# Two layers of a hybrid attention encoder: which of the engines beside TensorE splits the weights, scales the softmax rows and multiplies the norm

## The chip, the cores and the metric

The kernel runs on one core of one Trainium2 chip. The metric is the device time of one execution in microseconds (us). A core has TensorE (PE: matrix products, whose results lie in PSUM; PEld: its weight loads), VectorE (DVE), ScalarE (ACT), GpSimd (POOL) and SyncE (SP), which here issues the DMAs. Each engine works through its own queue in order, and engines wait for each other by semaphores.

## The reference

Batch 1, 512 rows, width 1024, two layers, all in f32. Cut to what matters:

```python
for l in range(DEPTH):
    mod = (silu(c) @ w_ada[l] + b_ada[l]).reshape(B, 9, D_MODEL)
    h = rms_norm(x) * (1 + mod[1]) + mod[0]
    x = x + 0.5 * mod[2] * swiglu(h, w_gate, w_up, w_down)              # first FFN
    h = rms_norm(x) * (1 + mod[4]) + mod[3]
    qa, ka, va, ub, qc, kc, vc, f, g = split(h @ w_in)                  # the mixer
    ya = attention(norm(qa), norm(ka), va, bias by distance, own + 8 chunks of 64)   # 8 heads of 64
    yb = trailing-window means of ub, minus ub, through w_pool
    yc = attention(norm(qc), norm(kc), vc, bias cumsum(log_sigmoid(f)), causal)      # 8 heads of 64
    x = x + mod[5] * (sum_n sigmoid(g_n) * (y_n @ w_branch[n])) @ w_out
    h = rms_norm(x) * (1 + mod[7]) + mod[6]
    x = x + 0.5 * mod[8] * swiglu(h, w_gate, w_up, w_down)              # second FFN
```

## The kernel before

Activations lie transposed: 128 channels on the partitions, 512 rows of the sequence as columns. To hold f32 precision every operand is split into a high part of a shorter type (fp32r) and a low part (`lo = value - hi`), and each product is three matmuls (`triple`, L119 to L121: high by high, high by low, low by high). So every weight chunk (128x1024 f32, 512 KB, DMA by SP) goes through `wchunk`: ACT casts the high part (`whi`, L268), and one engine subtracts for the low part (`wlo`, L270). `LO_SHARE = 1` gives the subtraction to POOL for the chunks loaded during the two attentions and to DVE elsewhere; `= 0` gives all to DVE there.

A layer is first FFN, mixer, second FFN. Each of the six begins with an RMS norm (`Norm`) in two halves of 256 columns. The squares are summed on ACT and POOL; PE sums over partitions; DVE makes the inverse root by three Newton steps (`rsqrt`, L276 to L284); PE spreads it over the partitions (`rb`, in PSUM), and ACT copies that to SBUF (`rbs`, L353). Then come eight pieces a half (`piece`): multiply by the inverse root (DVE from PSUM for three of eight, L360; POOL from `rbs` for five, L362), ACT's high part `hhi` (L364), DVE's low part `hlo` (L365). The products that follow read `hhi` and `hlo`.

In the mixer come the projections (`proj`), attention A, attention C, the pooling branch, the gates and the output. The query and key projections (`proj_qk`) end in a norm by head: DVE sums squares, `rsqrt` on 128x32, then for each of four row blocks a 128x512 multiplication by the inverse root (L665, two on POOL and two on DVE), then transposes on PE (`turn`).

An attention (`attention`) goes head by head, four query blocks of 128 each, in four steps:

- `logits`: PE products (L777, L778); DVE adds the bias strip and takes the row maximum (L781); ACT's exponential with row sums (L785); DVE reciprocal (L787); DVE scales the probabilities by it (`t<-t,rs`, L788).
- `turn`: PE transposes the scaled rows (L800), ACT copies the high part (L804), DVE subtracts the low part (L805).
- `weigh`: PE multiplies with the values (L822, L823); ACT and DVE add the halves (L826, L827), then `split_to` (L375 on ACT, L376 on DVE) writes the two parts of `y`.
- The strips of C come by DMA for a head ahead; POOL adds the causal mask to their diagonal blocks (L763).

Between these steps PE is given other products ("filler": projections and gates). What stands where is decided when the program is built: `pe[0]` counts PE time, `later(delay, fn)` notes a step to be emitted when `pe[0]` passes its due time, and `poll()` emits what is due. `LAG_T`, `LAG_V`, `STEP`, `TURN` are such delays. Tiles of one name share few buffers (`t1` has two, `t2` three, `strip` two), so that a step may wait until an older tile is read.

Of the kernel before, what the change touches and what calls it, by code (L numbers as in the profile page):

```python
# [15 lines left out]
F32 = mybir.dt.float32  # L16
# [3 lines left out]
ALU = mybir.AluOpType  # L20
# [20 lines left out]
def encoder_kernel(tc, xT, c, w_ada, b_ada, gains, w_gate, w_up, w_down, w_qkv, w_f, w_ubg,  # L41
# [22 lines left out]
    def st(shape, dt, tag, bufs):  # L64
        return sb.tile(shape, dt, tag=tag, bufs=bufs, name=nm(tag))
# [205 lines left out]
        return hi, lo  # L271


    def rsqrt(v, n):
        jt = st([P, n], I32, "nt_j", 2)
        nc.vector.tensor_scalar(jt, v.bitcast(I32), -0.5, 1597463007.0, op0=ALU.mult, op1=ALU.add)  # L276
        y = jt.bitcast(F32)
        for _ in range(3):
            q = st([P, n], F32, "nt_q", 1)
            u = st([P, n], F32, "nt_u", 1)  # L280
            z = st([P, n], F32, "nt_z", 2)
            nc.vector.tensor_tensor(q, y, y, op=ALU.mult)
            nc.vector.scalar_tensor_tensor(u, q, -0.5, v, op0=ALU.mult, op1=ALU.mult)  # L283
            nc.vector.scalar_tensor_tensor(z, u, 1.5, y, op0=ALU.add, op1=ALU.mult)  # L284
            y = z
        return y

    def xd(d):
        return x_blocks[d // 2][:, d % 2, :]
# [4 lines left out]
    class Norm:  # L294
# [10 lines left out]
        def sq(self, d, hs):  # L305

            cols = slice(0, T) if hs is None else slice(hs * HALF, (hs + 1) * HALF)
            x = xd(d)[:, cols]
            n = cols.stop - cols.start
            if d == 0:  # L310
                nc.scalar.activation(self.ssum[:, cols], x, AF.Square)
            elif d < KD - 1:
                q = t1(T)[:, :n]
                nc.scalar.activation(q, x, AF.Square)  # L314
                nc.gpsimd.tensor_tensor(self.ssum[:, cols], self.ssum[:, cols], q, op=ALU.add)  # L315
            else:
                self.work[hs] = st([P, 3 * HALF], F32, "strip", 2)
                w = self.work[hs][:, :HALF]
                nc.scalar.activation(w, x, AF.Square)
                nc.vector.tensor_tensor(w, w, self.ssum[:, cols], op=ALU.add)  # L320
            if d % 2 == 0 and self.xa[d // 2] is None:
                self.xa[d // 2] = blk(self.xtag, F32)
            nc.scalar.activation(self.xa[d // 2][:, d % 2, cols], x, AF.Identity, scale=apre[:, self.l, self.s, d:d + 1])
# [20 lines left out]
        def back_start(self, hs, bank):  # L344
            if self.state[hs] > 1:
                return
            self.front(hs, bank)
            self.state[hs] = 2
            w = self.work[hs]
            rb = bank((P, HALF))  # L350
            mm(rb, ones, w[:, HALF:2 * HALF], start=True, stop=True)
            rbs = w[:, 2 * HALF:3 * HALF]
            nc.scalar.copy(rbs, rb)  # L353
            cols = slice(hs * HALF, (hs + 1) * HALF)

            def piece(d):
                b = modc[:, self.l, 3 * self.s, d:d + 1]
                t = self.xa[d // 2][:, d % 2, cols]
                if d in ON_DVE:
                    nc.vector.tensor_tensor(t, rb, t, op=ALU.mult)  # L360
                else:
                    nc.gpsimd.tensor_tensor(t, rbs, t, op=ALU.mult)  # L362
                hi = hhi[:, d, cols]
                a_ins = nc.scalar.activation(hi, t, AF.Identity, bias=b)  # L364
                v_ins = nc.vector.scalar_tensor_tensor(hlo[:, d, cols], t, b, hi.bitcast(F32),  # L365
                                                       op0=ALU.add, op1=ALU.subtract)
                gate["scalar"], gate["vector"] = a_ins.ins, v_ins.ins
                last["norm"] = v_ins.ins

            self.pieces[hs] = [lambda d=d: piece(d) for d in range(KD)]  # L370
            for d in range(KD):
                later(STEP * d, lambda d=d: self.pieces[hs].pop(0)() if len(self.pieces[hs]) == KD - d else None)
# [59 lines left out]
    FRONT, BACK, FRONT1, BACK1 = 8, 24, 16, 28  # L432
    FRONT2, BACK2 = 16, 28
    STEP = 3
    ON_DVE = (0, 3, 6)


    class Ffn:
# [205 lines left out]
    def proj_qk(l, col, gcol, is_q, res, pre=None, norm=None):  # L644
        lows = []
        qs = []

        def evac(t, a):
            if t == 0:
                qs.extend((st([P, NT, T], F32, "ptb", 2), st([P, NT, H], F32, "qss", 1)))  # L650
            qn, ss = qs
            nc.scalar.copy(qn[:, t, :], a)
            sq = t2(T)
            nc.scalar.activation(sq, a, AF.Square)  # L654
            nc.vector.tensor_reduce(ss[:, t, :], sq.rearrange("p (h d) -> p h d", h=H), axis=AX.X, op=ALU.add)

        yield from proj(l, col, evac, pre, norm)
        qn, ss = qs
        v = st([P, NT * H], F32, "nt_v32", 2)
        nc.vector.tensor_scalar(v, ss.rearrange("p t h -> p (t h)"), 1.0 / HD, EPS, op0=ALU.mult, op1=ALU.add)  # L660
        r = rsqrt(v, NT * H)
        for t in range(NT):
            q3 = qn[:, t, :].rearrange("p (h d) -> p h d", h=H)
            eng = nc.vector if t % 2 else nc.gpsimd
            eng.tensor_tensor(q3, q3, r[:, t * H:(t + 1) * H].unsqueeze(2).to_broadcast([P, H, HD]), op=ALU.mult)  # L665

        def turn(p):
            pt = mmt()
            for t in range(NT):
                nc.tensor.transpose(pt[:, t * P:(t + 1) * P], qn[:, t, p * P:(p + 1) * P], ident)  # L670
            pe[0] += 2.2
            b = blk("b")
            if is_q:
                lows.append(blk("b"))
            first, second = slice(0, HD), slice(HD, P)
            for odd, (own, other) in enumerate(((first, second), (second, first))):
                dst = b[:, odd, :]
                gc = gcol[own, :]
                nc.scalar.activation(dst[own, :], pt[own, :], AF.Identity, scale=gc)
                low = dst[other, :]  # L680
                if is_q:
                    nc.scalar.activation(low, pt[own, :], AF.Identity, scale=gc)
                    nc.gpsimd.memset(lows[p][other, odd, :].bitcast(F32), 0.0)
                    low = lows[p][own, odd, :]
                nc.vector.scalar_tensor_tensor(low, pt[own, :], gc, dst[own, :].bitcast(F32),
                                               op0=ALU.mult, op1=ALU.subtract)
            res.append((b, lows[p]) if is_q else b)

        todo = [lambda p=p: turn(p) for p in range(4)]
        turns.append(todo)  # L690

        def ready(p):
            if len(todo) >= 4 - p:
                if heads[0] < (Q_GATE if is_q else K_GATE)[p]:
                    later(8, lambda: ready(p))
                else:
                    while len(todo) >= 4 - p:
                        todo.pop(0)()

        for p in range(4):  # L700
            later(TURN + 12 * p, lambda p=p: ready(p))

    turns = []
    heads = [H]
    TURN = 52
    Q_GATE, K_GATE = (2, 2, 4, 4), (6, 6, 8, 8)

    def finish_turns(upto=3):
# [57 lines left out]
    def attention(qs, ks, vs, strip, ys, filler, budget, group):  # L766
# [4 lines left out]
        def logits(h, i, strips):  # L771
            p, off = divmod(h, 2)
            (q, ql), k = qs[p], ks[p]
            odd = h % 2
            n = (i + 1) * P
            s = mmt()
            mm(s[:, :n], q[:, odd, i * P:(i + 1) * P], k[:, odd, :n], start=True, stop=False)  # L777
            mm(s[:, :n], ql[:, odd, i * P:(i + 1) * P], k[:, odd, :n], start=False, stop=True)  # L778
            lg = t1(T)[:, :n]
            mx = st([P, 1], F32, "mx", 4)  # L780
            nc.vector.tensor_tensor_reduce(out=lg, in0=s[:, :n], in1=strips[i], scale=-1.0, scalar=BIG,  # L781
                                           op0=ALU.add, op1=ALU.min, accum_out=mx)
            pr = t2(T)[:, :n]
            sm = st([P, 1], F32, "sm", 4)
            nc.scalar.activation(pr, lg, AF.Exp, bias=mx, scale=-1.0, accum_out=sm)  # L785
            rs = st([P, 1], F32, "rs", 4)
            nc.vector.reciprocal(rs, sm)  # L787
            nc.vector.tensor_scalar(pr, pr, rs, None, op0=ALU.mult)  # L788
            pe[0] += 0.5 * (i + 1.5)
            later(LAG_T, lambda: turn(h, i, pr), group)  # L790

# [18 lines left out]
        def weigh(h, half, pt):  # L810
# [14 lines left out]
            yl = t1(T)[:, :HALF]  # L825
            nc.scalar.copy(yl[rows, :], o[other, :])  # L826
            nc.vector.tensor_tensor(yl[rows, :], o[rows, :], yl[rows, :], op=ALU.add)  # L827
            split_to(y[rows, 0, cols], y[rows, 1, cols], yl[rows, :])
            pe[0] += 1.0 * nj

        for h in range(H):
# [194 lines left out]
                    residual_tail(d, hs, o, modc[:, l, 5, d:d + 1], nxt)  # L1026

    FILL_A, FILL_C = 9.5, 9.0
    LO_SHARE = 1

    phases = []
    for l in range(L):
# [64 lines left out]
```

## Time and profile before

| what | value |
|---|---|
| runs (3) | median 2491.94 us, 2489.65 to 2494.43 |
| profiled execution | 2496.94 us, span 2495.0 us |
| PE busy | 2429.8 us of the span (97%), 11898 matmuls |
| DVE busy | 1378.6 us (55%), 2424 instructions |
| ACT busy | 983.6 us (39%), 1644 instructions |
| POOL busy | 380.7 us (15%), 377 instructions |
| granted TensorE clock, mean | 0.998 |

Busy time is the sum of an engine's shown instructions. Matmuls are pipelined: a shown matmul of 128x512 lasts longer than the distance from its start to the next one's, so "97%" overstates how full PE is, and an idle time of PE in front of a matmul understates what the wait cost. In lines such as `PE mm L800 <- DVE t L788: 9.1, 8, 2.1` the columns are the idle time of PE in us that ended with that release, the number of such waits, and the longest. In a row of stretches come its length, then the busy time of PE, PEld, DVE, ACT and POOL (with their instructions), the granted clock, the share of the DMA engines and GB/s. In the timeline: start, duration, engine, line, operation, output and input, count, and in brackets the idle time before and what ended it.

### The profile page before, as it was taken

To read this page: it belongs to the slowest core of one execution; us is meant where nothing else is said; L and a number is where in the kernel's file an instruction comes from. 1 tells how busy PE (TensorE), PEld (TensorE's weight loads), DVE (VectorE), ACT (ScalarE), POOL (GpSimd) and SP (SyncE) were. 2 spreads that over 40 slices of the span, in tenths; PEclk is the share of its full clock that TensorE was granted. 3 is DMA by queue.
4 is the path that set the end of the run, shared out by engine and by line. 5 is a ranking of instruction groups with operands and counts; after the bars stand their busy time and mean duration, and the time that the engine had idled before them with its cause. 6 is when DMAs were issued, how large, how long until landed. Compare 5 with 4: busy or idle time off the path is not lost. (4 is left out here: it accounts for less than half of the span.)

```text
span 2495.0 us, 30866 instructions
## 1 busy us (share of the span) xinstructions
PE 2429.8 (97%) x11898; PEld 2030.3 (81%) x11898; DVE 1378.6 (55%) x2424; ACT 983.6 (39%) x1644; POOL 380.7 (15%) x377
## 2 busy tenths in 40 slices
PE   7999999989999999999999999999999999999999
PEld 5888888767788898888888888977777888888888
DVE  8655536788753465555365543467787434533332
ACT  5322235677532442223333222356765334422231
POOL 2000003343322220000110000124332322100000
PEclk9999999999999999999999999999999999999999
DMA  7655542223323425555335533323233233232322
GB/s 276 224 186 199 180 141 80 85 72 96 104 89 110 146 99 193 178 207 181 119 114 191 190 114 99 126 78 92 67 105 99 93 115 130 69 101 93 102 93 93
DMA packets 116263, 320.02 MB, mean 128 GB/s; under 512 B 11122, under 2 KB 13298, under 8 KB 116116
## 3 DMA queue, kind: packets, MB, share of 16 engines
q1 hardware_dynamic: 114962, 313.86, 37.3%
q0 software_dynamic: 1152, 4.19, 0.4%
q8 instruction: 93, 1.52, 0.2%
q14 instruction: 54, 0.44, 0.1%
q10 hardware_dynamic: 2, 0.00, 0.0%
HBM read 311.64 MB, written 6.38 MB: 127 GB/s over the span
## 5 line engine op out<-in xcount | busy, mean ns | idle before, releaser
L268 ACT CAST whi<-raw 128x1024 fp32r<-128x1024 f32 (+1 forms) x395 | 411.8, 1046 | 1090.9 <-PE acc L120 416.7
L270 DVE TENSOR_TENSOR wlo<-raw,whi 128x1024 fp32r<-128x1024 f32 x339 | 419.1, 1239 | 519.5 <-ACT whi L268 507.5
L121 PE MATMUL mm<-hhi,wlo 128*128 128x512 f32 x1304 | 507.4, 389 | 0.4 <-DVE wlo L270 0.4
L119 PE MATMUL mm<-hhi,whi 128*128 128x512 f32 x1304 | 507.6, 389 | 0.0
L120 PE MATMUL mm<-hlo,whi 128*128 128x512 f32 x1304 | 507.3, 389 | 0.0
L119 PE MATMUL acc<-b,whi 128*128 128x512 f32 (+1 forms) x960 | 355.9, 371 | 0.0
L121 PE MATMUL acc<-b,wlo 128*128 128x512 f32 (+1 forms) x960 | 353.4, 368 | 0.0
L120 PE MATMUL acc<-b,whi 128*128 128x512 f32 (+1 forms) x960 | 353.4, 368 | 0.0
L121 PEld LDWEIGHTS mm<-hhi,wlo 128*128 128x128 f32 x1304 | 244.7, 188 | 51.5 <-DVE wlo L270 0.9
L119 PEld LDWEIGHTS mm<-hhi,whi 128*128 128x128 f32 x1304 | 245.1, 188 | 50.8
L120 PEld LDWEIGHTS mm<-hlo,whi 128*128 128x128 f32 x1304 | 244.8, 188 | 50.9
L197 DVE CUSTOM_DVE_ANT_0 v<-v,b,badac 128x1024 f32<-128x1024 f32 x144 | 189.3, 1316 | 40.3 <-DMA v<-in_w_ada_dram 40.0
L121 PEld LDWEIGHTS acc<-b,wlo 128*128 128x128 f32 x960 | 180.9, 188 | 29.6
L120 PEld LDWEIGHTS acc<-b,whi 128*128 128x128 f32 x960 | 181.0, 189 | 29.3 <-DVE b L376 0.3
L119 PEld LDWEIGHTS acc<-b,whi 128*128 128x128 f32 x960 | 181.0, 189 | 28.8
L119 PE MATMUL acc<-hhi,whi 128*128 128x512 f32 x480 | 191.7, 401 | 1.7 <-ACT hhi L564 1.7
L120 PE MATMUL acc<-hlo,whi 128*128 128x512 f32 x480 | 188.5, 393 | 1.1 <-DVE hlo L567 1.1
L121 PE MATMUL acc<-hhi,wlo 128*128 128x512 f32 x480 | 188.9, 393 | 0.5 <-POOL wlo L270 0.4
L462 DVE TENSOR_TENSOR t<-mm,t 128x512 f32<-128x512 f32 x86 | 59.5, 691 | 210.0 <-PE mm L121 205.9
L270 POOL TENSOR_TENSOR wlo<-raw,whi 128x1024 fp32r<-128x1024 f32 (+1 forms) x56 | 132.5, 2370 | 172.1 <-ACT whi L268 137.3
L119 PE MATMUL acc<-whi,hhi 128*128 128x512 f32 x336 | 137.6, 409 | 4.9 <-ACT t L654 3.7
L120 PE MATMUL acc<-wlo,hhi 128*128 128x512 f32 x336 | 131.8, 392 | 0.0
(235 smaller groups left out, 3473.3 us busy)
## 6 DMA issues: line engine op xcount, KB each, us to landing
v<-in_w_ada_dram SPq DMA_DIRECT2D x144, 512.0 KB, 4.5
raw<-in_w_down_dram SPq DMA_DIRECT2D x88, 512.0 KB, 3.7
raw<-in_w_up_dram SPq DMA_DIRECT2D x82, 512.0 KB, 3.5
raw<-in_w_gate_dram SPq DMA_DIRECT2D x79, 512.0 KB, 3.5
raw<-in_w_ubg_dram SPq DMA_DIRECT2D x56, 512.0 KB, 3.5
raw<-in_w_qkv_dram SPq DMA_DIRECT2D x42, 512.0 KB, 3.6
raw<-in_w_branch_dram SPq DMA_DIRECT2D x24, 512.0 KB, 3.7
raw<-in_w_out_dram SPq DMA_DIRECT2D x16, 512.0 KB, 3.6
```

The source lines that it names most:

```text
L119: mm(o, lh, rh, start=start, stop=False)
L120: mm(o, lh, rl, start=False, stop=False)
L121: mm(o, ll, rh, start=False, stop=stop)
L197: dot = nc.vector.tensor_tensor_reduce(out=raw, in0=raw, in1=silc[0], scale=1.0, scalar=badac[:, l, j, d:d + 1], op0=ALU.mult, op1=ALU.add ...
L268: nc.scalar.copy(hi, raw)
L270: lo_eng.tensor_tensor(lo, raw, hi.bitcast(F32), op=ALU.subtract)
L462: nc.vector.tensor_tensor(pr, pu, sg, op=ALU.mult)
```

## The change

Six edits:

1. `LO_SHARE` goes from 1 to 0: the 48 subtractions of weights' low parts during the attentions move from POOL to DVE.
2. The scaling of the softmax rows (128 instructions, L788, in the new file L799) moves from DVE to POOL.
3. The low part of `y` in `weigh` (64 instructions, 64x256; L376, now L840) moves from DVE to POOL.
4. All multiplications of the RMS norms are made by DVE from PSUM (now L362); POOL's form and ACT's copy `rbs` go, and the `strip` tile of the norm is a third smaller.
5. The norm of queries and keys is made wholly on DVE (now L672),
6. and emitted as eight pieces 5 units of PE's count apart (`PACE`), not in one run.

```diff
-    def rsqrt(v, n):
+    def rsqrt_steps(v, n):
...
         for _ in range(3):
+            yield y
...
-                self.work[hs] = st([P, 3 * HALF], F32, "strip", 2)
+                self.work[hs] = st([P, 2 * HALF], F32, "strip", 2)
...
-            rbs = w[:, 2 * HALF:3 * HALF]
-            nc.scalar.copy(rbs, rb)
...
-                if d in ON_DVE:
-                    nc.vector.tensor_tensor(t, rb, t, op=ALU.mult)
-                else:
-                    nc.gpsimd.tensor_tensor(t, rbs, t, op=ALU.mult)
+                nc.vector.tensor_tensor(t, rb, t, op=ALU.mult)
...
-            eng = nc.vector if t % 2 else nc.gpsimd
-            eng.tensor_tensor(q3, q3, r[:, t * H:(t + 1) * H].unsqueeze(2).to_broadcast([P, H, HD]), op=ALU.mult)
+            r = norm_of["r"][:, t * H:(t + 1) * H].unsqueeze(2).to_broadcast([P, H, HD])
+            nc.vector.tensor_tensor(q3, q3, r, op=ALU.mult)
...
-        todo = [lambda p=p: turn(p) for p in range(4)]
+        todo = [first, step, step, step] + [lambda t=t: scale(t) for t in range(NT)]
+        todo += [lambda p=p: turn(p) for p in range(4)]
         turns.append(todo)
+        for n in range(8):
+            later(PACE * n, lambda n=n: todo.pop(0)() if len(todo) == 12 - n else None)
...
-            nc.vector.tensor_scalar(pr, pr, rs, None, op0=ALU.mult)
+            nc.gpsimd.tensor_scalar(pr, pr, rs, None, op0=ALU.mult)
...
-            split_to(y[rows, 0, cols], y[rows, 1, cols], yl[rows, :])
+            nc.scalar.copy(y[rows, 0, cols], yl[rows, :])
+            nc.gpsimd.tensor_tensor(y[rows, 1, cols], yl[rows, :], y[rows, 0, cols].bitcast(F32), op=ALU.subtract)
...
-    LO_SHARE = 1
+    LO_SHARE = 0
```

How this shows in the queues, at two places. DVE, first half of the mixer's norm in layer 0 (`v` is the tile that is multiplied, `mm` the spread inverse root, `xv` the residual), before:

```order
L360 TENSOR_TENSOR v_422_2488<-mm_2871,v_422_2488 128x256
L360 TENSOR_TENSOR v_425_2523<-mm_2871,v_425_2523 128x256
L360 TENSOR_TENSOR v_461_2767<-mm_2871,v_461_2767 128x256
L365 SCALAR_TENSOR_TENSOR hlo<-v_422_2488,modc,hhi 128x256
L425 SCALAR_TENSOR_TENSOR xv_97<-acc_2548,modc,xv_97 128x256
L365 SCALAR_TENSOR_TENSOR hlo<-v_425_2523,modc,hhi 128x256
```

and after:

```order
L362 TENSOR_TENSOR v_422_2488<-mm_2871,v_422_2488 128x256 x2
L362 TENSOR_TENSOR v_425_2523<-mm_2871,v_425_2523 128x256 x2
L365 SCALAR_TENSOR_TENSOR hlo<-v_422_2488,modc,hhi 128x256 x2
L425 SCALAR_TENSOR_TENSOR xv_97<-acc_2548,modc,xv_97 128x256
L365 SCALAR_TENSOR_TENSOR hlo<-v_425_2523,modc,hhi 128x256 x2
L425 SCALAR_TENSOR_TENSOR xv_97<-acc_2549,modc,xv_97 128x256
L362 TENSOR_TENSOR v_458_2732<-mm_2871,v_458_2732 128x256 x2
```

Four multiplications stand ahead of the first `hlo` now, and POOL's five are gone from beside it. POOL, early heads of attention C in layer 0, before:

```order
L763 TENSOR_TENSOR strip_5242<-strip_5242,cmask 128x128 x3
L763 TENSOR_TENSOR ssum_5106<-ssum_5106,cmask 128x128
L763 TENSOR_TENSOR strip_5399<-strip_5399,cmask 128x128 x3
L270 TENSOR_TENSOR wlo_5441<-raw_5438,whi_5440 128x1024
L763 TENSOR_TENSOR ssum_5244<-ssum_5244,cmask 128x128
L763 TENSOR_TENSOR strip_5552<-strip_5552,cmask 128x128 x3
```

and after (`t` are the softmax rows, `rs` the reciprocal sums, `b` is `y`; L774 is the old L763):

```order
L774 TENSOR_TENSOR strip_5397<-strip_5397,cmask 128x128 x3
L840 TENSOR_TENSOR b_5088<-t_1059_5194,b_5088 64x256
L799 TENSOR_SCALAR t_1064_5213<-t_1064_5213,rs_5216 128x512
L774 TENSOR_TENSOR ssum_5242<-ssum_5242,cmask 128x128
L799 TENSOR_SCALAR t_1077_5254<-t_1077_5254,rs_5257 128x128
L840 TENSOR_TENSOR b_5088<-t_1081_5268,b_5088 64x256
L799 TENSOR_SCALAR t_1092_5299<-t_1092_5299,rs_5302 128x256
L799 TENSOR_SCALAR t_1099_5327<-t_1099_5327,rs_5330 128x384
L840 TENSOR_TENSOR b_5088<-t_1105_5353,b_5088 64x256
L774 TENSOR_TENSOR strip_5550<-strip_5550,cmask 128x128 x3
```

The subtraction of a weight is gone from POOL; the scaling of a head's last and longest block (128x512) stands behind the mask of the strip two heads later and behind a low part of `y`. On DVE the same stretch has one `wlo` more for each that POOL lost, and none of L788.

More of the change, by code (lines that the diff above doesn't have):

```diff
@@ L285, in rsqrt @@
             y = z
-        return y
+        yield y
+    def rsqrt(v, n):
+        return list(rsqrt_steps(v, n))[-1]
     def xd(d):
@@ L434, in encoder_kernel @@
     STEP = 3
-    ON_DVE = (0, 3, 6)
     class Ffn:
@@ L658, in proj_qk, with first, step, scale @@
         qn, ss = qs
[L659 to L662, printed above, removed]
+        norm_of = {}
+        def first():
+            v = st([P, NT * H], F32, "nt_v32", 2)
+            nc.vector.tensor_scalar(v, ss.rearrange("p t h -> p (t h)"), 1.0 / HD, EPS, op0=ALU.mult, op1=ALU.add)
+            norm_of["steps"] = rsqrt_steps(v, NT * H)
+            next(norm_of["steps"])
+        def step():
+            norm_of["r"] = next(norm_of["steps"])
+        def scale(t):
             q3 = qn[:, t, :].rearrange("p (h d) -> p h d", h=H)
-            eng = nc.vector if t % 2 else nc.gpsimd
-            eng.tensor_tensor(q3, q3, r[:, t * H:(t + 1) * H].unsqueeze(2).to_broadcast([P, H, HD]), op=ALU.mult)
+            r = norm_of["r"][:, t * H:(t + 1) * H].unsqueeze(2).to_broadcast([P, H, HD])
+            nc.vector.tensor_tensor(q3, q3, r, op=ALU.mult)
         def turn(p):
@@ L705, in encoder_kernel @@
     TURN = 52
+    PACE = 5
     Q_GATE, K_GATE = (2, 2, 4, 4), (6, 6, 8, 8)
```

## The prediction

> **What bounds the kernel now.** I read the engines' shares first, then the distance between matmuls in a stretch without waits, then PE's waits, then the stretches in which the waits lie, then the timeline around the longest.
>
> ```profile
> PE 2429.8 (97%) x11898; PEld 2030.3 (81%) x11898; DVE 1378.6 (55%) x2424; ACT 983.6 (39%) x1644; POOL 380.7 (15%) x377
> 839.82 0.39 PE L120 MATMUL acc<-hlo,whi 128*128 128x512 f32 x1
> 840.04 0.39 PE L121 MATMUL acc<-hhi,wlo 128*128 128x512 f32 x1
> 840.27 0.39 PE L119 MATMUL acc<-hhi,whi 128*128 128x512 f32 x1
> ```
>
> PE sets the time, and none of its matmuls changes. Unhindered, a 128x512 matmul starts 0.225 us after the last ((840.27 - 839.82) / 2), though it is shown as 0.39 long; so a wait of PE costs about 0.16 us more than the idle time in its row. All that the change can gain is PE's waits and clock, all that it can lose is new waits.
>
> ```profile
> PE mm L800 <- DVE t L788: 9.1, 8, 2.1
> PE mm L823 <- DVE ptb L805: 6.8, 7, 1.2
> PE acc L121 <- DVE hlo L365: 4.3, 2, 2.2
> PE acc L119 <- ACT t L654: 3.7, 4, 1.3
> PE mm L777 <- DVE t L827: 3.3, 5, 1.1
> PE mm L800 <- DVE nt_z L284: 2.5, 2, 1.2
> PE mm L777 <- DVE mx L781: 2.4, 4, 1.0
> PE mm L777 <- DVE b L685: 1.7, 2, 0.8
> PE acc L119 <- ACT hhi L364: 1.7, 2, 0.8
> PE mm L120 <- DVE hlo L365: 1.1, 3, 0.4
> 380.00:405.00 25.00, 22.01 (x118) 18.32 (x118) 19.39 (x52) 11.14 (x28) 11.40 (x17) 0.93 0.16 55
> 440.00:700.00 260.00, 241.18 (x1256) 194.66 (x1255) 203.66 (x502) 170.10 (x374) 87.90 (x82) 1.00 0.29 92
> 885.00:910.00 25.00, 23.95 (x190) 23.00 (x190) 20.37 (x53) 13.81 (x29) 10.76 (x13) 1.00 0.05 15
> ```
>
> The waits that the change can touch stand here. They lie at the mixer's norm (380 to 405), in the two attentions (440 to 700) and, small, at the FFN norms (885 to 910), and again in layer 1. DVE is busy 204 of 260 us in the attentions, POOL 88. Why DVE is late there, the timeline tells:
>
> ```profile
> 386.38 3.46 POOL L362 TENSOR_TENSOR v<-strip,v 128x256 f32<-128x256 f32 x5
> 386.25 3.88 DVE L365 SCALAR_TENSOR_TENSOR hlo<-v,modc,hhi 128x256 fp32r<-128x256 f32 x1
> 390.19 0.61 PE L121 MATMUL acc<-ptb,hlo 128*128 128x512 f32 x1 [2.16 <-DVE hlo L365]
> 610.88 2.35 POOL L270 TENSOR_TENSOR wlo<-raw,whi 128x1024 fp32r<-128x1024 f32 x1
> 611.07 2.44 DVE L788 TENSOR_SCALAR t<-t,rs 128x512 f32<-128x512 f32 x1
> 613.57 0.66 PE L800 MATMUL mm<-ident,t 128*128 128x128 f32 x4 [2.12 <-DVE t L788]
> 497.11 2.35 DVE L660 TENSOR_SCALAR nt_v<-qss 128x32 f32<-128x32 f32 x1
> ```
>
> One `hlo` takes 3.88 us, as long as five POOL instructions beside it; one 128x512 scaling takes 2.44, as long as the `wlo` beside it, and even a 128x32 operation 2.35. These are DVE instructions whose operands all lie in SBUF. Those that read PSUM do not stretch so. So PE waits for DVE, and DVE is held by POOL. The Trainium skill, "SBUF — State Buffer", section "SBUF: two separate sides", has this as an exclusive lock: a DVE instruction with two SBUF inputs, or in a two-port mode, and a GpSimd instruction share a port pair, and whichever starts first keeps it to its end. The 3.88 us agree.
>
> **The change part by part.** The durations:
>
> ```profile
> L788 DVE TENSOR_SCALAR t<-t,rs x128: 276/420/2729, 469.6 to 1922.9; 128x128 f32<-128x128 f32 x32, 128x256 f32<-128x256 f32 x32, 128x384 f32<-128x384 f32 x32, 128x512 f32<-128x512 f32 x32
> L365 DVE SCALAR_TENSOR_TENSOR hlo<-v,modc,hhi x48: 469/484/3884, 386.2 to 1640.4; 128x256 fp32r<-128x256 f32 x48
> L362 POOL TENSOR_TENSOR v<-strip,v x30: 712/741/1016, 386.4 to 1638.1; 128x256 f32<-128x256 f32 x30
> L360 DVE TENSOR_TENSOR v<-mm,v 128x256 f32<-128x256 f32 x15 | 5.4, 418 | 3.4 <-ACT strip L353 3.4
> L270 POOL TENSOR_TENSOR wlo<-raw,whi x56: 1800/2400/2881, 13.9 to 1901.5; 128x1024 fp32r<-128x1024 f32 x48, 128x768 fp32r<-128x768 f32 x8
> L270 DVE TENSOR_TENSOR wlo<-raw,whi 128x1024 fp32r<-128x1024 f32 x339 | 419.1, 1239 | 519.5 <-ACT whi L268 507.5
> L376 DVE TENSOR_TENSOR b<-t,b 64x256 fp32r<-64x256 f32 x64 | 37.2, 581 | 11.1 <-ACT b L375 9.9
> L665 DVE TENSOR_TENSOR ptb<-ptb,nt_z x16: 691/1112/1533, 421.2 to 1779.9; 128x512 f32<-128x512 f32 x16
> L683 POOL MEMSET b<- 64x512 f32 x32 | 17.0, 530 | 3.8 <-PE mm L778 2.5
> L866 POOL TENSOR_TENSOR strip<-strip 128x512 f32<-128x512 f32 x12 | 13.0, 1080 | 0.5
> ```
>
> *Norm multiplications to DVE.* Ahead of the first `hlo` stand four of L360's kind (4 x 0.418 = 1.67 us) where three stood (1.25), and ACT's copy no longer comes first. But that `hlo` then takes 0.47 (its shortest) and not 3.88: it ends about 3 us earlier, more than the 2.16 that PE waited. So both waits of 4.3 go, with 0.32 beside them; so does the slow clock behind them (0.93 over 25 us is 1.75 us of clock, in each layer, 3.5). The other waits of the norm (1.7 and 1.1 in five, 3.6 with 0.16 each) go by half, since `hhi` now waits for one engine's multiplications in a row: 1.8. An FFN norm shows 1.05 us without PE (25.00 - 23.95); half of three is 1.5. Gain: 4.6 + 3.5 + 1.8 + 1.5 = 11.4 us. Bounds: 5, if something else comes 2 us late at the same place, and 14.
>
> *Scaling, `wlo` and query norm in the attentions.* With `wlo` off POOL nothing of 2.4 us is left there to hold DVE. The waits on L788, on L805 (queued on DVE behind a held L788) and on the late `nt_z` come to 9.1 + 6.8 + 2.5 and 17 x 0.16, 21.1 us. Not all goes, since the scaling has a new queue. No row shows POOL's scaling. The least it can take for 128x512 is the 0.53 of a memset of as many columns, the most the 1.08 of an addition of two inputs; I take 0.62, nearer to the memset, as only one tensor is read. The Trainium skill, "GPSIMD Engine Reference", section "4.1 Engine selection", speaks against elementwise work on GpSimd: half of VectorE's speed with two inputs, about its speed with one. The `wlo` rows, 2.40 against 1.24, agree for two; of one input no run here shows it; by the page 128x512 would take about 0.49, and the sum would not move by 1 us.
>
> ```profile
> 609.44 1.47 POOL L763 TENSOR_TENSOR strip<-strip,cmask 128x128 f32<-128x128 f32 x3 [4.22 <-DMA strip<-fv_dram]
> 620.71 0.68 DVE L781 CUSTOM_DVE_ANT_0 t<-mm,ssum 128x512 f32<-128x512 f32 x1
> 621.28 1.29 POOL L763 TENSOR_TENSOR strip<-strip,cmask 128x128 f32<-128x128 f32 x3 [7.46 <-DMA strip<-fv_dram]
> 622.48 2.73 DVE L788 TENSOR_SCALAR t<-t,rs 128x512 f32<-128x512 f32 x1
> ```
>
> In attention C the longest scaling stands on POOL behind a strip's mask, which waits for a DMA, and behind L840. At 609.44 that makes 1.47, then at most 0.71 (L362's shortest, which has as many columns), then 0.62: ready at 612.24, where before it was ready at 613.51 and PE began to wait at 611.45. So 0.8 of 2.12 us stays there; at 621.28 it is ready at 623.9 where 625.21 made no wait. I let two thirds of the L788 waits go (6.9 of 10.4), three quarters of those on L805 and `nt_z` (8.1 of 10.7): 15 us. Of the waits on L827, L781 and L685 (7.4 and 11 x 0.16, 9.2) a third, 3, as DVE is only relieved: 48 x 1.24 = 59.5 us of `wlo` come, of L788 at least 54 (128 x 0.42, its median, without the holds) and of L376 37.2 go. ACT's 3.7 (L654) stays. Bounds for this part: 30, all of it, and 6.
>
> *What is new.* Each `wlo` on DVE holds what stands behind it by up to 1.24 us. DVE had room for 56 us in 260, so for most of 48 nothing late stands behind; one in eight at 0.6 makes 3.6 us. Low parts of `y` on POOL (0.41 to 0.71 for 0.58) are read late, by the branch products, but hold a buffer of `t1` that ACT's copy and L781 want; with them POOL's queue: 1.4. Together 5; bounds 0 and 17 (below).
>
> *Query norm on DVE, in pieces.* 16 instructions come to DVE at 0.69 (11 us), 16 get shorter by 0.42 (7 us); the pieces let row maxima pass between. Nothing on PE's path but what is counted at `nt_z`.
>
> The sum: -11.4 - 15 - 3 + 5 = -24.4. The profiled execution took 2496.94, so 2472.5; it lies 5.0 above the median of the runs, 2491.94. Against the median: 2467.5, said as 2468. By the lock rule, a `wlo` on DVE could in turn hold a scaling on POOL up to 1.24 us; 48 of them fill 11% of 520 us, so some 14 of 128 scalings would be held 0.6 each, and the sum would be at most 8 us less gain.
>
> **Rivals.**
> - *Half the gain.* DVE's queue is what PE waits for, and `wlo` takes L788's place in it: if a third of the 48 come in front of a row maximum or a low part that PE wants at once, 16 x (1.24 - 0.16) = 17 us are new, not 5: 2480. For it speaks that L827 and L781 make waits without any held L788; against it that DVE loses twice what it takes on.
> - *Slower.* POOL's chain in attention decides: strip's DMA, three masks, L840, scaling, and behind it L840 and ACT's exponentials by the two buffers of `t1`. If the chain from 621.28 ends after 625.21, PE waits longer than before. With 1.29 and 0.71 that takes a scaling above 1.9 us, nearly twice the highest row. If it came to 2.9, each of 32 heads would lose 1 us beside the 15 not gained: -11.4 - 3 + 5 + 32 = +23, 2515. It decides from about 0.5 us a head on.
> - *No change.* The waits at L788 and L805 only end in DVE's name, and ACT's exponential or its high part (L804), ready just before, makes PE wait nearly as long; then only the norm's gain stays, and a third of `wlo` at its price eats that: -11.4 + 12 makes about 2492. Against it: at 611.07 and 622.48 L788 ran 2.0 and 2.3 us above its median of 0.42, and behind the first of them PE waited.
>
> **How the numbers follow.** What this kernel's measurement can tell from no change is about 0.2%, 5 us (the three runs spread over 4.8). The forecast, 2455 to 2479: 0.60. Half the gain, 2479 to 2487: 0.20. More than forecast, below 2455 (all waits of the list go, none come): 0.06. No change, 2487 to 2497: 0.07. Slower: 0.07. So faster 0.86, same 0.07, slower 0.07. The range leaves out the slower cases, most of no change and the lowest: 2450 to 2488.
>
> **What would show it.** Right: `hlo` at the mixer's norm near 0.47 us and no PE wait of 2 us there, with the granted clock of that stretch near 1.00; no DVE instruction above 1.3 us in the attentions; waits on L788's successor below 4 us in all; POOL's 128x512 scaling between 0.5 and 1.1. Wrong: a scaling above 1.9 us; waits of PE on row maxima (old L781) or on ACT that grow by more than 10 us; a `wlo` that is held long itself; PE at half clock behind new waits.

## The result, and the profile after

The changed kernel took 2471.98 us (median of 6 runs, 2469.75 to 2473.67), the kernel before 2492.53 (6 runs, 2489.65 to 2494.43): ratio 0.9918, 95% interval 0.9907 to 0.9928. That is 20.5 us faster; 24.4 had been forecast. The mechanism held, but several terms of the sum were far off, in opposite directions, so the near agreement is in part luck. The runs show that two of the six edits together cost 18 us.

The profiled execution (2469.75 us, span 2467.7) has these shares:

```profile
PE 2420.8 (98%) x11898; PEld 2027.6 (82%) x11898; DVE 1313.8 (53%) x2346; ACT 979.8 (40%) x1634; POOL 399.7 (16%) x455
```

POOL lost 48 subtractions of 2.41 us and is still busier than before. PE's waits, those on POOL among them:

```profile
PE mm L811 <- POOL t L799: 13.2, 18, 1.8
PE mm L552 <- ACT ssum L548: 4.6, 1, 4.6
...
PE acc L119 <- ACT t L653: 3.6, 6, 1.3
PE mm L788 <- DVE mx L792: 3.2, 6, 1.1
PE mm L788 <- DVE t L838: 3.1, 5, 1.1
PE mm L788 <- DVE b L692: 1.8, 2, 0.9
...
PE acc L120 <- POOL b L840: 1.3, 2, 0.7
```

(New line numbers: L811 are the transposes of the softmax rows, L799 their scaling, L788 the products of the logits, L838 the sum of halves, L840 the low part of `y`.) The waits on `hlo` L365, on `hhi` L364, on the low parts of the transposed rows and on `nt_z` are gone. In the place of L788's 9.1 us stand 13.2 us on the same scaling, now on POOL.

The stretches, in the same columns as before:

```profile
380.00:405.00 25.00, 25.00 (x139) 21.25 (x139) 20.95 (x66) 12.15 (x27) 8.11 (x16) 1.00 0.20 66
440.00:700.00 260.00, 247.04 (x1288) 200.48 (x1287) 174.03 (x437) 169.42 (x374) 124.97 (x155) 1.00 0.31 95
885.00:910.00 25.00, 25.00 (x166) 23.05 (x165) 17.42 (x41) 11.73 (x19) 0.00 (x0) 1.00 0.35 114
```

At the mixer's norm PE now runs without a gap and at a clock of 1.00, where it was busy 22.01 of 25 us at 0.93. In layer 0's attentions DVE's busy time fell by 30 us and POOL's rose by 37. DVE at the mixer's norm:

```profile
384.59 1.42 DVE L362 TENSOR_TENSOR v<-mm,v 128x256 f32<-128x256 f32 x4
385.99 0.98 DVE L365 SCALAR_TENSOR_TENSOR hlo<-v,modc,hhi 128x256 fp32r<-128x256 f32 x2
```

Two `hlo` take 0.98 us where one took 3.88. POOL's new groups by shape, three of five, with busy time, mean ns of one, and idle time before and what ended it:

```profile
L840 POOL TENSOR_TENSOR b<-t,b 64x256 fp32r<-64x256 f32 x64 | 57.6, 900 | 60.2 <-ACT b L839 59.0
L799 POOL TENSOR_SCALAR t<-t,rs 128x512 f32<-128x512 f32 x32 | 50.1, 1566 | 42.6 <-DVE rs L798 30.1 <-DVE mx L792 3.7 <-PE mm L834 3.1
...
L799 POOL TENSOR_SCALAR t<-t,rs 128x128 f32<-128x128 f32 x32 | 19.2, 600 | 133.7 <-DVE rs L798 130.8 <-PE mm L789 2.8
```

A scaling of 128x512 takes 1.57 us on POOL. In the kernel before DVE did it in 0.49 unhindered (the median of this shape), and in 1.08 on the mean with all its holds.

### The profile page after: what moved, and what is told of

Same layout as the page of the kernel before. It is cut to its first block, busy times and chain, and to the rows that moved or that the text cites. A ratio compares the mean times of both kernels' runs of the same rounds, so it can differ in the third digit from the quotient of the medians.

```text
span 2467.7 us, 31105 instructions
## 1 busy us (share of the span) xinstructions
PE 2420.8 (98%) x11898; PEld 2027.6 (82%) x11898; DVE 1313.8 (53%) x2346; ACT 979.8 (40%) x1634; POOL 399.7 (16%) x455
## 4 chain that ended last, share of the span: by engine, by line
PE 86%; DVE 5%; ACT 5%; POOL 2%; issue 2%; DMA 0%; DVEq 0%; POOLq 0%; ACTq 0%
PE acc L119 14%; PE acc L120 14%; PE acc L121 14%; PE mm L121 14%; PE mm L119 14%; PE mm L120 14%; POOL t L799 1%; PE mm L811 1%; ACT whi L268 1%; ACT b L686 1%; DVE wlo L270 1%; ACT b L689 1%; DVE v L197 1%; POOL b L840 1%; ACT t L796 1%
## 5 line engine op out<-in xcount | busy, mean ns | idle before, releaser
L270 DVE TENSOR_TENSOR wlo<-raw,whi 128x1024 fp32r<-128x1024 f32 x387 | 475.7, 1231 | 532.7 <-ACT whi L268 520.3
L799 POOL TENSOR_SCALAR t<-t,rs 128x128 f32<-128x128 f32 (+3 forms) x128 | 138.4, 1084 | 251.1 <-DVE rs L798 220.3
L121 PE MATMUL acc<-whi,hlo 128*128 128x512 f32 x336 | 132.1, 393 | 0.0
```

The costliest lines, as they stand in the source:

```text
L121: mm(o, ll, rh, start=False, stop=stop)
L270: lo_eng.tensor_tensor(lo, raw, hi.bitcast(F32), op=ALU.subtract)
L799: nc.gpsimd.tensor_scalar(pr, pr, rs, None, op0=ALU.mult)
```

## The experiments

Times are medians, each beside runs of the kernel before on the same chip (2492.2 to 2492.8). An interval of a ratio is 0.0010 to 0.0016 to either side, 3 to 4 us.

**Scaling alone back on DVE** (`scale_dve`).

```diff
-            nc.gpsimd.tensor_scalar(pr, pr, rs, None, op0=ALU.mult)
+            nc.vector.tensor_scalar(pr, pr, rs, None, op0=ALU.mult)
```

> The changed kernel with the softmax scaling alone put back on DVE. Theory A: what the attentions lost went by way of POOL's 2.4 us subtractions that held DVE; the scaling on POOL adds a wait of its own (1.57 us for 128x512, PE waits 13.2 us in 18 on it) and gives back most of the gain. Then PE's waits on the scaling fall below 4 us and the time to 2460 (2456 to 2464). Rival B: DVE has no room for the scaling beside the 48 subtractions; the waits move to DVE's row maxima and low parts, and the time is 2472 or more.

2465.52 us, ratio 0.989 (0.9876 to 0.9904): 6.5 us faster than the changed kernel. PE's waits on the scaling fell to 1.4 us in 5, as theory A said, but the gain is half of A's and the time outside its range. One thing that stands against the rest shows in the timeline, DVE's row first and POOL's rows under it:

```profile
499.35 1.36 DVE L799 TENSOR_SCALAR t<-t,rs 128x384 f32<-128x384 f32 x1
...
499.24 0.80 POOL L840 TENSOR_TENSOR b<-t,b 64x256 fp32r<-64x256 f32 x1 [8.60 <-ACT b L839]
499.98 0.52 POOL L690 MEMSET b<- 64x512 f32 x1
```

The scaling, 0.42 us when free, ends 0.2 us after the second of the two POOL instructions: with `y`'s low parts on POOL the old holding of DVE is back in small. How much of the missing gain this makes is not shown by this run.

**Low parts of `y` alone back on DVE** (`y_dve`): `nc.gpsimd` to `nc.vector` in L840.

> The changed kernel with the low parts of y alone put back on DVE. Theory A: on POOL they stand ahead of the scalings (0.9 us each, 64 of them) and hold ACT's evacuation by 12.9 us; back on DVE the scalings come earlier and the time falls by 3 us, to 2469. Rival B: they are off PE's path on either engine: 2472, within 1 us. Rival C: DVE's queue gets longer by 64 x 0.42 us and PE waits more: 2474 or more.

2466.05 us, ratio 0.9891 (0.9877 to 0.9905), 5.9 us faster than the changed kernel. The price was thus not 1.4 us, as the prediction had it, and is twice theory A's. A's way is not borne out either, since the scalings on POOL did not come sooner for PE:

```profile
PE mm L811 <- POOL t L799: 13.5, 14, 1.8
...
PE mm L788 <- DVE mx L792: 1.4, 4, 0.4
```

PE waits on the scaling 13.5 us where it was 13.2. What fell are its waits on row maxima, from 3.2 to 1.4 us, and those on L840 itself, 1.3 us, are gone.

**Both back on DVE** (`scale_y_dve`): what is left is the weights' low parts and all norm work on DVE.

> The changed kernel with scaling and low parts of y both back on DVE: what is left of the change is the weights' low parts and all norm work on DVE. Theory A: the parts add, since they lie in different stages: weights' low parts alone gave 22.2 us, the norm alone 12.1; together 34, so 2458 (2455 to 2461), and neither kernel of the comparison is as fast. Rival B: the two share a part of their gain, or the query norm on DVE takes some back: 2463 or more.

2453.83 us, ratio 0.9847 (0.9833 to 0.986): the fastest version, 18.2 us under the changed kernel and 38 to 39 under the one before, a little faster than theory A's range. The two returned parts are worth more together (18.2) than one by one (6.5 and 5.9). The engines' shares, then PE's waits on logits and scaling, then the stretch:

```profile
PE 2417.8 (99%) x11898; PEld 2027.3 (83%) x11898; DVE 1375.3 (56%) x2538; ACT 979.8 (40%) x1634; POOL 209.9 (9%) x263
```

```profile
PE mm L788 <- DVE t L838: 2.6, 4, 1.1
...
PE mm L811 <- DVE t L799: 1.3, 6, 0.3
...
PE mm L788 <- DVE mx L792: 0.6, 2, 0.3
```

```profile
440.00:700.00 260.00, 253.69 (x1322) 207.21 (x1322) 210.54 (x544) 174.31 (x380) 32.97 (x65) 1.00 0.32 97
```

DVE is busier here than in the kernel before (210.5 against 203.7 of 260 us), and yet PE is busy 253.7 us of this stretch where it was 241.2: DVE's load was not the trouble, its holds were.

**Norm alone** (`norm_only`): the kernel before, the multiplications of the norms on DVE from PSUM, without ACT's copy.

> The kernel before with the norm's multiplications alone moved to DVE (from PSUM, without ACT's copy). Theory A: by the distances of matmuls the norms of the changed kernel lost 16.6 us less than before, of it 9.8 at the two mixer norms and 6.8 at the three FFN norms, and this edit alone makes it: 2476 (2474 to 2478). Rival B: the terms of the prediction, 11.4 us: 2481. Rival C: a part of it comes from other edits, since POOL and DVE are busy with a weight's low part around the norm: 2484 or more.

(The distances are counted from each matmul's start to the next one's, beyond what is usual for its shape; summed over the span they are 27.3 us less in the changed kernel's profiled execution, as its span is.) 2480.16 us, ratio 0.9944 (0.9931 to 0.9957): 12.1 us between the medians, 10.7 to 17.2 by the interval. That holds both the prediction's term and the 16.6, and leaves out theory C. The median lies at B's time and above A's range; the norms' distances in this run's trace fell by the same 16.6 us as in the changed kernel's. So this edit alone makes the norms' gain. Why the trace says more than the medians is taken up below.

**Weights' low parts alone** (`wlo_only`): the kernel before with `LO_SHARE = 0`.

> The kernel before with the 48 subtractions of weights' low parts in the attentions alone moved to DVE; scaling and low parts of y stay on DVE as well. Theory A: the holding of DVE by POOL was the cost, and DVE has room: the attentions lose 15 us less, 2477 (2473 to 2481), with no scaling on DVE above 1 us outside the query norms. Rival B: with 60 us more on DVE its queue becomes what PE waits for, and nothing is gained: 2490 or more.

2470.07 us, ratio 0.9908 (0.9894 to 0.9922): 22.2 us, as much as the whole change or a little more, from one number. That is theory A, and 7 us more than it said. The scaling's durations, PE's waits, and `hlo` in this run's timeline:

```profile
L788 DVE TENSOR_SCALAR t<-t,rs x128: 276/412/753, 468.0 to 1895.5; 128x128 f32<-128x128 f32 x32, 128x256 f32<-128x256 f32 x32, 128x384 f32<-128x384 f32 x32, 128x512 f32<-128x512 f32 x32
```

```profile
PE acc L121 <- DVE hlo L365: 4.3, 2, 2.2
...
PE mm L800 <- DVE t L788: 2.1, 7, 0.5
...
PE mm L822 <- DVE ptb L805: 1.6, 2, 0.8
...
PE mm L777 <- DVE mx L781: 0.6, 2, 0.3
```

```profile
386.09 3.88 DVE L365 SCALAR_TENSOR_TENSOR hlo<-v,modc,hhi 128x256 fp32r<-128x256 f32 x1
380.00:405.00 25.00, 22.01 (x124) 18.35 (x123) 21.08 (x55) 12.71 (x29) 11.43 (x17) 1.00 0.18 65
```

The longest scaling is 0.75, not 2.73; the waits on L788 fell from 9.1 to 2.1 us, and of those on L805, 6.8 at L823, 1.6 are left at another matmul. The norm's stall of 2.2 us stands here as before, `hlo`'s 3.88 us with it: the two parts have different places. But behind this stall the clock stays at 1.00, where it was 0.93 in the same stretch before.

**Weights' low parts and norm** (`wlo_norm`): both of the last two on the kernel before.

> The kernel before with two edits alone, weights' low parts and norm multiplications on DVE; the query norm stays in one run, half of it on POOL. Theory A: 2458, as with the query norm in pieces on DVE, since no wait of PE on the query norm's own result showed. Rival B: with the two multiplications of 1.5 us on POOL left, DVE is held there, and it is 2 to 4 us slower than with the query norm on DVE: 2460 to 2462.

2454.99 us, ratio 0.9852 (0.9839 to 0.9866). The parts add: 12.1 + 22.2 = 34.3 against 37.8 between the medians, and the interval is 33 to 40. It is within 1.2 us of `scale_y_dve`, which has the query norm on DVE and in pieces too, so that beside these two parts edits 5 and 6 add nothing that can be told.

**Query norm in one run** (`qnorm_one`): the changed kernel, its eight pieces called at once.

> The changed kernel with the query and key norm emitted in one run on DVE, as before the change, and not in eight pieces. Theory A: nothing of it is on PE's path, 2472 within 1.5 us. Rival B: twelve small steps and four multiplications, about 5 us of DVE in a row, stand in front of row maxima and low parts; 8 norms with 0.5 us each make 2476 or more.

2474.22 us, ratio 0.9928 (0.9914 to 0.9941), 2.2 us above the changed kernel, between the two theories and inside the intervals: not settled. PE's waits on the scaling are 15.5 us in 18 there, against 13.2 in 18.

**Weights' low parts back on POOL, scaling there too** (`wlo_pool`): the changed kernel with `LO_SHARE = 1`.

> The changed kernel with the weights' low parts back on POOL, which scales the softmax rows as well. Theory A: each subtraction of 2.41 us stands ahead of scalings on POOL, whose lateness PE sees; 48 of them, half in front of a scaling that PE wants, make 30 to 60 us beside the changed kernel: 2500 to 2530, slower than before. This is the prediction's slower rival, made real. Rival B: with DVE free of its longest instructions nothing there is held, and POOL, busy about 60% in the attentions, keeps up: 2472 or less.

2498.13 us, ratio 1.0022 (1.0012 to 1.0031): slower than before, although the norms have their gain. This is the prediction's slower rival at a lower price (5 us and not 23), and 26 us more than the changed kernel, just under theory A's 30:

```profile
PE mm L811 <- POOL t L799: 23.8, 17, 3.1
PE mm L833 <- ACT pta L815: 5.5, 2, 2.8
```

The granted clock has a part in it: its mean is 0.9945 over the ten runs, and 0.9977 over the changed kernel's six. Over 2500 us that is some 8 of the 26 us, an estimate from these means.

**Scaling on POOL, written with two tensors** (`scale_tt`): the mis-sized price tried by itself.

```diff
-            nc.gpsimd.tensor_scalar(pr, pr, rs, None, op0=ALU.mult)
+            nc.gpsimd.tensor_tensor(pr, pr, rs.to_broadcast([P, n]), op=ALU.mult)
```

> The changed kernel, with POOL's scaling written as a multiplication of two tensors (the reciprocal spread over the row) and not by a column. Theory A: the price of the instruction on POOL was what the prediction mis-sized (1.57 us for 128x512, where POOL's addition of two tensors takes 1.08); at 1.08 PE's waits on the scaling fall from 13.2 to about 6 us, and the time to 2466 (2463 to 2469). Rival B: an instruction with two tensors is caught by the subtractions on DVE, as the low parts of y are (0.73 alone, 1.28 to 2.02 beside one), and holds DVE in turn; nothing gained, 2471 or more.

2463.65 us, ratio 0.9887 (0.9872 to 0.9902), 8.3 us faster than the changed kernel, as theory A said.

```profile
L799 POOL TENSOR_TENSOR t<-t,rs 128x512 f32<-128x512 f32 x32 | 33.2, 1039 | 47.8 <-DVE rs L798 45.1 <-DVE nt_z L286 2.4
```

```profile
PE mm L811 <- POOL t L799: 6.8, 10, 1.2
```

With 1.04 us for 1.57, at the same place in the same queue, half of PE's waits on the scaling go. So half of them came by the duration of the instruction.

**A third buffer for `t1`** (`y_t1`, with the control `best_t1`): `bufs` of `t1` 3 for 2, `NB` 16 for 17; scaling on DVE in both, the low parts of `y` on POOL in the first and on DVE in the control.

> Low parts of y on POOL, scaling on DVE, with three buffers of t1 for two (and 16 blocks b for 17, to make room). With two buffers this took 2465.5, and 2453.8 with the low parts on DVE. Theory A: the 11.7 us come by the buffers of t1, which POOL's late subtraction keeps from ACT (15.2 us waited) and from the row maxima (3.8); with a third they go, and it is within 2 us of the same kernel with low parts on DVE. Rival B: they come by the port, POOL holding DVE's scaling (up to 1.37 us) and DVE's subtractions holding POOL; then 8 us or more stay between the two.

> The control: scaling and low parts of y on DVE, with three buffers of t1 and 16 blocks b. Theory A: the third buffer does nothing where nobody waits for one: 2454 within 2 us. Rival B: one block b less delays loads and costs 3 us or more; then the run with the low parts on POOL is to be compared with this one only.

2462.17 (ratio 0.988, 0.9863 to 0.9896) and 2457.26 (0.9862, 0.9847 to 0.9877). The control is 3.4 us slower than `scale_y_dve`, which theory B puts down to one block `b` less, so only these two are compared: 4.9 us lie between them, where 11.7 lay between the same two with two buffers. Neither theory holds alone, then. Some 7 of the 11.7 went with the third buffer (with two, ACT's activation of the gates waited 15.2 us in 8 for L840; with three it does not wait for it). Each of these differences is good to about 4 us, so the share is rough, and whether the rest is the holding between POOL and DVE was not separated.

## Why the prediction was right, and where not

*The mechanism held.* PE waited for DVE, and DVE was held by POOL. With `wlo` gone from POOL no scaling on DVE exceeds 0.75 us, and nearly all of the waits behind it go. With the norm's multiplications gone from POOL `hlo` takes 0.48 us, and PE's stall behind it goes. These two parts alone make the kernel 38 us faster (`wlo_norm`). The sum came near the measured time for a poorer reason: its terms missed in both directions.

*The norm.* The forecast was 11.4 us; it is 12.1 between the medians when done alone and 15.1 on top of the other part. Two terms inside it were off, against each other, so that the nearness of the sum is luck. The FFN norms were put at 1.5, half of PE's idle time in one window times three; by the distances of matmuls they gave 6.8, so the idle time showed only a part of what they cost. And the half clock behind the mixer's stalls, 3.5 us, was counted as lost in every execution. It stood at both mixer norms of the profiled execution: in the first the clock is 0.66 over the 5 us from 390, which is 1.7 us, and matmuls of 128x512 start 0.43 us apart where 0.225 is usual. But the trace before has four waits of 2.1 us in the mixers, and behind the one at 613.57 the clock is 1.00; in `wlo_only` the same stall of 2.16 us has a clock of 1.00 behind it in layer 0 and of 0.66 in layer 1. And taking the stall away did not raise the mean clock of the runs: 0.9986 over the five of `norm_only`, 0.9987 over the nine before that stand beside them. Without the 3.4 us of clock the trace's 16.6 becomes 13.2, near the 12.1 of the medians. The terms for the waits at the mixer's norm were right: 4.6 + 1.8, where the distances without the clock give 9.8 - 3.4 = 6.4.

*The attentions*: the forecast was -15 - 3 + 5, 13 us of gain; the rest of 20.5 after the norm's 12.1 is 8. Here too mis-sized terms stand against each other.

First, the weights' low parts gained more than said. Each `wlo` on DVE was to hold what stands behind it, 3.6 us in all (the step "What is new"). Nothing of it shows: `wlo_only`, with 58.7 us more of `wlo` on DVE (477.8 against 419.1), gains 22.2 us, against 18 for the waits that I let go. Of the three smaller waits (L827, L781 and L685) a third was to go, and 7.4 became 5.0 us; but it was not an even third, since those on row maxima (L781) fell from 2.4 to 0.6. These were mostly made by the holds, further down DVE's queue.

Second, the scaling on POOL: 0.62 us was taken for 128x512, 1.08 was the upper end, and it is 1.57. The end was an addition of two tensors, thought to be dearer than any instruction with one; but the multiplication by a column takes longer than a multiplication of two tensors of the same size (1.04). So the chain that I worked out for attention C (1.47 + 0.71 + 0.62 after the strip's DMA) was short by 0.95 us and more, and PE's waits on the scaling did not fall but rose to 13.2. The sentence from the Trainium skill, "GPSIMD Engine Reference", section "4.1 Engine selection", that one-input work runs there at about VectorE's speed, does not hold for this instruction: 1.57 against 0.49 us. Its advice, to leave such work on VectorE, does: `scale_y_dve`.

Third, the low parts of `y` on POOL, 1.4 us in the sum, cost 5.9 us beside the scaling on POOL and 11.7 beside the scaling on DVE. I had named the way (a buffer of `t1` that ACT and the row maxima want), and given it no price of its own; the third buffer of `t1` takes some 7 of the 11.7 away. That L840 stands ahead of the scalings on POOL is not what it costs, as PE's waits on them stayed at 13.5 without it. L840 is also lengthened by DVE's `wlo`: in 14 of 64 cases it takes 0.5 us or more above its median, each time beside one:

```profile
626.47 1.78 POOL L840 TENSOR_TENSOR b<-t,b 64x256 fp32r<-64x256 f32 x1
...
626.43 1.23 DVE L270 TENSOR_TENSOR wlo<-raw,whi 128x1024 fp32r<-128x1024 f32 x1 [0.51 <-ACT whi L268]
```

It started 0.04 us after the `wlo`, and ended 0.6 us after its end: 1.78 for an instruction whose median in this run is 0.73.

A part of the 18.2 us that the two moves cost together is clock: its mean is 0.9977 over the changed kernel's six runs and 1.000 in all four of `scale_y_dve`. Over 2470 us that makes some 5 us, an estimate from these means. The kernel before has 0.9988 over the thirty runs that stand beside the experiments, so by these means the change did not bring the gain in clock that the sum counted. In the changed kernel's trace such a stretch stands behind the wait of 1.78 us on POOL's scaling at 1806 (0.66 over 5 us).

*The signs.* `hlo` at 0.48, no wait of 2 us at the norm and its clock of 1.00 came as said; the longest DVE instruction in the attentions is a `wlo` of 1.35 where 1.3 was the limit. The two signs for POOL's scaling did not come: 13.2 us of waits and not under 4, and 1.57 us for 128x512, outside 0.5 to 1.1.

*The rivals.* "Slower" had its mechanism right and its place: POOL's chain in the attentions. Its point of decision, a scaling above 1.9 us, was not reached; 1.57 took back a part. "Half the gain" put the loss on DVE's queue, where it was not: waits on row maxima came to 3.2 us after 2.4. That a `wlo` on DVE holds a scaling on POOL, up to 8 us in the sum, did not come in the changed kernel, whose longest scaling is 1.62. That PE's wait would only change its name to ACT was not seen: PE's waits on ACT in the attentions are 3.6 us after and 3.7 before.

## What to carry to other kernels

Moving work off a busy engine is not the same as relieving it: read first whether its long instructions are long by themselves or held by a neighbour. A hold shows as a maximum far above the median in one group, with the neighbour's instruction ending just before (0.3 us at 611 and 622). Here one number (`LO_SHARE`) removed the larger part of the cause (22.2 us), and the two edits that lightened DVE further cost 18 us, since they put slow instructions on the path and new holds beside it. An instruction that no row of the trace shows on an engine deserves a trial before its price is bounded by relatives: "fewer inputs" was no bound.

## What was not expected of the hardware

- POOL's multiplication by a column, 600 ns for 128 columns and 1566 for 512, against 398 and 1039 for the same work with two tensors.
- The holds go both ways. DVE's `hlo` and scaling wait for POOL (3.88 and 2.73 us), and POOL's two-tensor subtraction waits for DVE's `wlo` (1.28 to 2.02 for 0.73).
- POOL's scaling by a column takes part in it only in some cases. Here it does not, though both instructions read and write the same memory:

```profile
500.74 1.24 POOL L799 TENSOR_SCALAR t<-t,rs 128x384 f32<-128x384 f32 x1 [1.40 <-DVE rs L798]
...
501.42 1.21 DVE L270 TENSOR_TENSOR wlo<-raw,whi 128x1024 fp32r<-128x1024 f32 x1
```

They overlap by 0.56 us, and neither is longer than elsewhere (the mean of this shape of the scaling is 1.24, that of `wlo` 1.23). It began before the `wlo`. In `qnorm_one` the order is the other way, a `wlo` at 501.51 and the same scaling at 501.76, and the scaling takes 2.06:

```profile
L798 POOL TENSOR_SCALAR t<-t,rs x128: 593/1085/2061, 464.8 to 1902.2; 128x128 f32<-128x128 f32 x32, 128x256 f32<-128x256 f32 x32, 128x384 f32<-128x384 f32 x32, 128x512 f32<-128x512 f32 x32
```

And a 128x32 operation on DVE (L285) takes 0.57 for 0.19 us beside a scaling that began 0.22 us before it, at 534.89 in the changed kernel. The Trainium skill, "SBUF — State Buffer", section "SBUF: two separate sides", counts any GpSimd instruction that reads this memory as a party to the lock, from its start to its end. The scaling at 501.76 agrees; the `wlo` at 501.42, which should have waited until 501.98, does not.
- What a wait of PE costs beyond its length is uneven. Behind three of the four waits of 2.1 us in the mixers before, and one of two in `wlo_only`, PE runs at half clock for some 3.4 us (1.7 us lost); behind all six waits of 2.7 us or more in `wlo_pool` it does. `scale_y_dve` has no wait above 1.3 us after the first 60 us and no such stretch until its last microseconds.
